# Another order of the constants' allocation in a two-layer encoder trunk

## The chip, the core and the metric

The kernel runs on one core of one Trainium2 chip. The metric is the device time of one execution in microseconds (us); three runs of the kernel before are shown as a median. The profile is of one further execution. TensorE is called PE, VectorE DVE, ScalarE ACT, GpSimd POOL and SyncE SP. PE's loads of the stationary operand have a row of their own, PEld.

## The reference

256 tokens of width 1024 go through two layers. The output is the token matrix, 256 x 1024, float32.

```python
for l in range(DEPTH):                       # DEPTH = 2
    x = x + 0.5 * swiglu(rms_norm(x, ffn1_norm[l]), ffn1_w1[l], ffn1_w3[l], ffn1_w2[l])   # D_FF = 2816
    h = rms_norm(x, mix_norm[l])
    z = h @ w_in[l]                          # 1024 x 6752, split into the inputs of three mixers and 3072 gates
    y_na  = neighborhood_attention(...)      # 8 heads
    y_gla = gla_bidirectional(...)           # 4 heads, gated linear attention in chunks of 64
    y_mla = mla_attention(...)               # 4 heads, low-rank q and kv
    mixed = (gt[:, :, 0] * (y_na @ w_br_na[l]) + gt[:, :, 1] * (y_gla @ w_br_gla[l])
             + gt[:, :, 2] * (y_mla @ w_br_mla[l]))
    x = x + mixed @ w_out[l]
    x = x + 0.5 * swiglu(rms_norm(x, ffn2_norm[l]), ffn2_w1[l], ffn2_w3[l], ffn2_w2[l])
```

## The kernel before

**Split products.** Each float32 operand of a large product is held as two float32r tiles, hi (a rounded copy, made on ACT) and lo (the rest, made on DVE by a subtraction). A product is three matmuls that add up in one bank of PSUM: hi by hi, hi by lo, lo by hi.

**The weight stream.** All weights stand in one list of units of up to 128 x 2048 elements (1 MB) in the order of use. SP loads a unit into one of three buffers `raw`; ACT (L138) and DVE (L144) split it in two halves into one of four buffers `hl`, where `hl[:, 0]` is hi and `hl[:, 1]` is lo. The split runs two units ahead of the matmuls. The order of everything is written out by hand: each function issues its matmuls through the helper `mm` (so they all have line 368) and calls `tick`, which emits a piece of the split and one step of each side task.

**The activations.** `xT` holds the transposed input of the next product: two blocks of 128 tokens (t), hi and lo, eight chunks of 128 features, 16 KB in each partition. It is rewritten after every residual addition (`norm_task`, `mix_task`). Nearly all other intermediate tiles come from a pool `s2` of 31 buffers of 2 KB.

**Which operand stands still.** This differs by stage, and in the rows of the profile `out<-in` the first name behind the arrow is the operand that streams, the second the one that stands still:

- `fform` (the upward half of the feed-forward, 80 calls with 16 pairs of matmuls each): `hl` stands still, 128 columns at a time, and `xT` streams. The first matmul of a pair streams hi and lo of both blocks (512 columns in four runs of 128), the second hi alone (256 columns). In the rows: `acc<-xT,hl`, 128x512 and 128x256.
- `tform` (the first columns of that half, where the norm is not ready yet): `xT` stands still, `hl` streams 256 columns.
- `wide_out` with `uT` (the downward half): `uT`, two buffers of `s2`, stands still, and `hl` streams 512 columns. In the rows: `acc<-hl,s`.
- `dense8` (the input projection of the mixers): `xT` stands still, `hl` streams 512 columns, or 408 in the four groups of gates. In the rows: `acc<-hl,xT`. The small products of the low-rank attention, `up_proj`, stand between them with their operand `cT` in `s2` (`ta<-hl,s`).
- `branch` (the three mixers' outputs): the same helper `burst` as `dense8`, but `yT`, from `s2`, stands still.
- `wide_out` with `X` (the output projection): the same helper as the downward half, but `xT` stands still.

```python
def burst(acc, lh, hl, ks, t, N, start, stop, k0=0):      # dense8: lh = X; branch: lh = yT
    n = len(ks)
    for i, k in enumerate(ks):
        a, b = (i + k0) * N, (i + k0 + 1) * N
        mm(acc, lh(0, k, t), hl[:, 0, a:b], start and i == 0, False)
        mm(acc, lh(0, k, t), hl[:, 1, a:b], False, False)
        mm(acc, lh(1, k, t), hl[:, 0, a:b], False, stop and i == n - 1)
```

**Where the tiles lie.** The pool `cst` hands out addresses in each partition one behind the other, in the order of its allocations, from byte 16512, which is 128 behind a multiple of 512. The pools of `raw`, `hl` and `s2` follow at 65536; all their buffers start on multiples of 512 bytes.

Of the kernel before, what the change touches and what calls it, by code (L numbers as in the profile page):

```python
# [6 lines left out]
F32 = mybir.dt.float32  # L7
F32R = mybir.dt.float32r
BF = mybir.dt.bfloat16
I32 = mybir.dt.int32  # L10
# [35 lines left out]
def body(tc, T):  # L46
# [3 lines left out]
    with ctx:  # L50
        ctx.enter_context(tc.manual_schedule())
        cst = ctx.enter_context(tc.tile_pool(name="cst", bufs=1))
# [17 lines left out]
        tr_t = lambda: bank("ta", 4)  # L70
        at_t = lambda: bank("ta", 4)

# [1 line left out]
        units = []  # L74
        for l in range(DEPTH):
            W = T["layers"][l]
# [91 lines left out]
                if st["hi"] < lim:  # L168
                    emit_hi()

# [1 line left out]
        tasks = []  # L172

        def step(tk):
# [24 lines left out]
            while not tk.done:  # L199
                step(tk)  # L200

# [1 line left out]
        x = cst.tile([128, 2, D], F32, name="x")  # L203
        idt = cst.tile([128, 128], F32, name="idt")
        xT = cst.tile([128, 2, 2, 8, 128], F32R, name="xT")
        gates = cst.tile([128, 2, 2048], F32, name="gates")
        rope = cst.tile([128, 2, 2, 64], F32, name="rope")
        am = cst.tile([128, 64], I32, name="am")
        aT = [cst.tile([128, 2, 2, 128], F32, name=f"aT{t}") for t in range(2)]
        gcol = cst.tile([128, 8], F32, name="gcol")  # L210
        mhalf = cst.tile([128, 16], F32, name="mhalf")
        ones = cst.tile([128, 1], F32, name="ones")
        zT = cst.tile([32, 2, 256], F32R, name="zT")

        def load_consts():
# [171 lines left out]
        def dense8(N, evac, pre=None, between=None):  # L387
            tks = []
            if pre is not None:
                ua, ub = unit(), unit()  # L390
                for t in range(2):
                    for h in range(2):
                        finish(pre[t, h])
                    acc = acc_t()
                    burst(acc[:, :N], X, ua, range(4), t, N, True, False)
                    tick(t == 0)
                    burst(acc[:, :N], X, ub, range(4, 8), t, N, False, True)
                    tks.append(drain(evac, t, acc))
                    tick()
                return tks  # L400
            accs = [acc_t(), acc_t()]
            for kh in range(2):
                u = unit()
                for t in range(2):
                    if kh == 0 and between:
                        between(t)
                    burst(accs[t][:, :N], X, u, range(4 * kh, 4 * kh + 4), t, N, kh == 0, kh == 1)
                    if kh:
                        tks.append(drain(evac, t, accs[t]))
                    tick()  # L410
            return tks
# [32 lines left out]
                for h in range(2):  # L444
                    mm(acc[h], lhs(1, u, kk, t), hl[:, 0, kk * 1024 + h * 512:kk * 1024 + h * 512 + 512], False, e)

# [1 line left out]
        def ffn(norms, after, prefetch, first=None, out=None):  # L448
            uT = {}

# [101 lines left out]

            wide_out(True, lhs, NCH, done)

# [1 line left out]
        def mixer(l, norms, after, prefetch):  # L556
            W = T["layers"][l]
            row, col, gup = params.pop(l)
# [2 lines left out]
            DVE.scalar_tensor_tensor(out=gqk_na, in0=col[:, 0:1], scalar=0.125, in1=col[:, 1:2],  # L561
                                     op0=ALU.mult, op1=ALU.mult)

            # ---- evacuations of the projections
            sg, cn, rl, nqk, nav, gvt, ssr = {}, {}, {}, {}, {}, {}, {}

            def pow_(ss, n):
# [90 lines left out]
                        nc.sync.dma_start(out=nav[j][64 * t + 32 * r:64 * t + 32 * r + 32, :],  # L658
                                            in_=v[64 * r + k0:64 * r + k0 + 32, :])

            # ---- shared by the two softmax attentions
            yT = {}

            def normalise(P, sums):
# [24 lines left out]
                        PE.transpose(ps[:, k, t, :], src[t][:, a:a + 128], idt)  # L689
                return ps.rearrange("p k t n -> p k (t n)")  # L690

            # ---- neighbourhood attention
            naT = {}

            def na_tr(nm, deps):
# [85 lines left out]
                            DVE.tensor_copy(PT, ps)  # L781
                    yield 1

            # ---- latent attention
            mq, mk, mv, mr = {}, {}, {}, {}

            def ev_uq(t, accs):
# [142 lines left out]
                            PTs[h] = p_trans(Ps.pop(h))  # L930
                    yield 1

            # ---- gated linear attention
            gqk = {}
            E, L, Y, dec = {}, {}, {}, {}

# [148 lines left out]
                    ysplit(ps.rearrange("p k n -> p (k n)"), "gla", j)  # L1085
                yield 1

            # ---- projections, with the three mixers running beside them
            m_tk = dense8(512, ev_m, norms)
            c_tk = spawn(c_task(m_tk), 1)  # L1090
            dense8(512, ev_gr)
# [99 lines left out]
                after(t, h)  # L1191
            wide_out(True, lhs, 4, done)

# [1 line left out]
        def spawner(ap, into, params_of=None):  # L1195
            G = []

            def f(t, h):
                into[t, h] = spawn(norm_task(t, h, G[0]), 1)

            def prefetch():
                G.append(load_gain(ap))
                if params_of is not None:
                    load_params(params_of)
            return f, prefetch
# [3 lines left out]
        for l in range(DEPTH):  # L1209
            W = T["layers"][l]  # L1210
            nm, n2 = {}, {}
            ffn(n, *spawner(W["gm"], nm, l), first=first if l == 0 else None)
            mixer(l, nm, *spawner(W["g2"], n2))
            if l + 1 < DEPTH:
                n = {}
                ffn(n2, *spawner(T["layers"][l + 1]["g1"], n))
            else:
                ffn(n2, None, lambda: None, out=T["out"])
# [14 lines left out]


def _rel_index():
    """Row offset, column offset and window test of (block, query, key) in the order of the bands."""
    j, q, p = np.arange(4)[:, None, None], np.arange(64)[:, None], np.arange(128)
    r, c = q % 4, 16 * j + q // 4
    k0 = np.clip(16 * j - 8, 0, 32)
    kr, kc = p // 32, k0 + p % 32  # L1240
    c0 = np.clip(c - 8, 0, 48)
    ok = (kc >= c0) & (kc < c0 + 16)
    dr = np.broadcast_to(kr - r + 7, ok.shape)
    dc = np.clip(kc - c + 15, 0, 30)
    return dr, dc, ok
# [14 lines left out]
def layout(inp):  # L1260
# [6 lines left out]
    j, i = np.arange(128)[:, None], np.arange(128)[None, :]  # L1267
    A["am"] = _tok((j % 64 > i)[:, :64].astype(np.int32))
    dr, dc, ok = _rel_index()
    for l in range(DEPTH):  # L1270
        p = f"l{l}_"
# [68 lines left out]
```

## Time and profile before

| what | value |
|---|---|
| median of 3 runs | 1270.34 us (1270.18 to 1270.63) |
| span of the profiled execution, first to last instruction | 1267.6 us |
| PE busy | 1253.1 us (99%), 7124 matmuls |
| PEld busy | 1074.4 us (85%) |
| DVE busy | 894.0 us (71%) |
| ACT busy | 711.9 us (56%) |
| POOL busy | 221.3 us (17%) |
| DMA | 228.34 MB, mean 180 GB/s |

The profiled execution has its span and no time of its own beside it; the median of the runs is 2.74 us longer than the span, which is the launch and the end around the instructions. Matmuls overlap: one begins while the one before it is still draining, so the duration of one (391 ns) is longer than the step from one start to the next. The step is read from the timeline, where a row that merges n matmuls of one kind gives the time from the first start to the last end: the step is that time less one duration, over n - 1.

### The profile page before, as it was taken

The numbers are of one execution on the slowest core, as the hardware profiler recorded it, in microseconds if no ns is written. First come the engines' busy times: TensorE is split into PE (matmuls) and PEld (weight loads), VectorE is DVE, ScalarE is ACT, GpSimd is POOL, SyncE is SP. The second block draws the span as 40 slices with busy tenths as digits, with TensorE's granted clock in tenths as the row PEclk, the third lists the DMA queues.
The fourth block names the chain that finished last, engine by engine and source line by source line (L and its number), as shares of the span: only waits on it lengthen the run. The fifth ranks groups of instructions, "written<-read, shape, count | busy, mean of one in ns | idle before, by whom it ended". The sixth has DMA issues, their size and how long they took to land.

```text
span 1267.6 us, 18330 instructions
## 1 busy us (share of the span) xinstructions
PE 1253.1 (99%) x7124; PEld 1074.4 (85%) x7124; DVE 894.0 (71%) x1382; ACT 711.9 (56%) x1315; POOL 221.3 (17%) x169
## 2 busy tenths in 40 slices
PE   8999999999999999999999999999999999999998
PEld 7888788889988898888898888888899788988887
DVE  5888736678766878886378886466886567788852
ACT  6555536667665366555365564356686644665541
POOL 0322101132011112220012220021322020122200
PEclk9999999999999999999999999999999999999999
DMA  7655644552543545556355556346526434555561
GB/s 301 222 180 187 241 158 158 203 194 87 196 166 133 200 166 185 185 196 232 133 186 203 195 195 235 113 173 225 167 90 207 163 134 170 196 199 182 186 230 34
DMA packets 37751, 228.34 MB, mean 180 GB/s; under 512 B 5712, under 2 KB 6864, under 8 KB 13088
## 3 DMA queue, kind: packets, MB, share of 16 engines
q1 hardware_dynamic: 37488, 227.09, 50.5%
q8 instruction: 56, 0.92, 0.3%
q14 instruction: 31, 0.25, 0.1%
q0 software_dynamic: 32, 0.07, 0.0%
q10 hardware_dynamic: 144, 0.00, 0.0%
HBM read 224.00 MB, written 1.05 MB: 178 GB/s over the span
## 4 chain that ended last, share of the span: by engine, by line
PE 88%; DVE 7%; ACT 4%; issue 1%; DMA 0%; DVEq 0%; ACTq 0%
PE acc L368 79%; DVE hl L144 6%; PE ta L368 6%; ACT hl L138 2%; ACT s L478 1%; PE ta L689 1%; PE ta L259 1%; DVE s L487 1%; PE ta L776 0%; DVE aT L1017 0%; PE ta L1172 0%; DMA gcol<-in_gcol 0%; PE ta L674 0%; ACT aT L1016 0%; PE ta L608 0%
## 5 line engine op out<-in xcount | busy, mean ns | idle before, releaser
L144 DVE TENSOR_TENSOR hl<-raw,hl 128x1024 fp32r<-128x1024 f32 (+2 forms) x422 | 568.0, 1385 | 101.7 <-ACT hl L138 91.4
L138 ACT ACTIVATE hl<-raw 128x1024 fp32r<-128x1024 f32 (+2 forms) x422 | 417.2, 1041 | 110.2 <-PE acc L368 93.5
L368 PE MATMUL acc<-xT,hl 128*128 128x512 f32 (+1 forms) x2768 | 475.6, 334 | 0.6 <-DVE s L479 0.6
L368 PEld LDWEIGHTS acc<-xT,hl 128*128 128x128 f32 x2768 | 417.8, 188 | 55.7 <-DVE s L479 0.9
L368 PE MATMUL acc<-hl,xT 128*128 128x512 f32 (+2 forms) x1728 | 369.0, 369 | 0.0
L368 PEld LDWEIGHTS acc<-hl,xT 128*128 128x128 f32 x1728 | 299.8, 188 | 45.7 <-issue 2.1
L368 PE MATMUL acc<-hl,s 128*128 128x512 f32 x1344 | 310.9, 391 | 1.5 <-DVE s L479 1.5
L368 PEld LDWEIGHTS acc<-hl,s 128*128 128x128 f32 x1344 | 250.8, 188 | 54.4 <-DVE s L479 1.9
L480 POOL TENSOR_TENSOR s<-s,rsb 128x512 f32<-128x512 f32 x80 | 111.8, 1397 | 355.7 <-DVE s L479 355.7
L489 ACT ACTIVATE s<-s 128x256 fp32r<-128x256 f32 x82 | 34.2, 418 | 172.4 <-DVE s L487 172.4
L479 DVE TENSOR_TENSOR s<-acc,s 128x256 f32<-128x256 f32 x158 | 59.6, 419 | 58.5 <-ACT s L478 58.5
L569 POOL TENSOR_TENSOR sm<-sm,mhalf 128x4 f32<-128x4 f32 (+2 forms) x24 | 36.7, 1531 | 202.7 <-DVE sm L573 196.0
L280 POOL TENSOR_TENSOR sm<-sm,mhalf 128x1 f32<-128x1 f32 x12 | 14.2, 1182 | 298.5 <-DVE sm L279 298.5
L478 ACT ACTIVATE s<-acc 128x256 f32<-128x256 f32 x158 | 50.6, 372 | 0.0
L242 ACT ACTIVATE s<-ta 128x512 fp32r<-128x512 f32 (+1 forms) x46 | 22.9, 531 | 39.9 <-PE ta L689 19.9
L243 DVE TENSOR_TENSOR s<-ta,s 128x512 fp32r<-128x512 f32 (+1 forms) x46 | 26.6, 604 | 24.4 <-ACT s L242 24.1
L368 PE MATMUL ta<-s,s 64*64 64x128 f32 (+3 forms) x720 | 41.0, 265 | 2.1 <-ACT s L1026 2.1
L368 PEld LDWEIGHTS ta<-s,s 64*64 64x64 f32 (+2 forms) x720 | 32.1, 144 | 12.4 <-issue 5.9
L262 ACT ACTIVATE xT<-ta,gain 128x128 fp32r<-128x128 f32 x80 | 22.8, 369 | 35.1 <-PE ta L259 35.1
L485 ACT ACTIVATE s<-s 128x256 f32<-128x256 f32 x82 | 34.2, 418 | 10.9 <-POOL s L480 0.2
L546 DVE SCALAR_TENSOR_TENSOR x<-acc,x 128x512 f32<-128x512 f32 (+1 forms) x20 | 11.3, 579 | 39.7 <-PE acc L368 39.7
L491 DVE TENSOR_TENSOR s<-s,s 128x256 fp32r<-128x256 f32 x82 | 34.0, 415 | 1.9 <-ACT s L489 1.9
(158 smaller groups left out, 652.4 us busy)
## 6 DMA issues: line engine op xcount, KB each, us to landing
raw<-in_l_f_w SPq DMA_DIRECT2D x130, 1024.0 KB, 4.8
raw<-in_l_in_g SPq DMA_DIRECT2D x16, 816.0 KB, 4.4
raw<-in_l_in_late SPq DMA_DIRECT2D x8, 1024.0 KB, 4.8
raw<-in_l_out SPq DMA_DIRECT2D x8, 1024.0 KB, 4.7
raw<-in_l_in_m SPq DMA_DIRECT2D x4, 1024.0 KB, 4.8
raw<-in_l_in_gr SPq DMA_DIRECT2D x4, 1024.0 KB, 4.8
raw<-in_l_in_r SPq DMA_DIRECT2D x4, 1024.0 KB, 4.8
raw<-in_l_in_nv SPq DMA_DIRECT2D x4, 1024.0 KB, 5.0
```

The lines of the kernel that those rows point to most:

```text
L138: ACT.activation(out=hls[j][:, 0, sl], in_=raws[j][:, sl], func=AF.Copy)
L144: DVE.tensor_tensor(out=hl[:, 1, sl], in0=r[:, sl], in1=hl[:, 0, sl].bitcast(F32), op=ALU.subtract)
L242: ACT.activation(out=hi, in_=ps, func=AF.Copy)
L243: DVE.tensor_tensor(out=lo, in0=ps, in1=hi.bitcast(F32), op=ALU.subtract)
L368: PE.matmul(out=out, lhsT=lhsT, rhs=rhs, start=start, stop=stop, skip_group_check=True)
L478: ACT.activation(out=g[:, j, :], in_=a[j][:, 256:], func=AF.Copy)
L479: DVE.tensor_tensor(out=g[:, j, :], in0=a[j][:, :256], in1=g[:, j, :], op=ALU.add)
L480: POOL.tensor_tensor(out=g, in0=g, in1=rb[:, None, :].to_broadcast([128, 2, 256]), op=ALU.mult)
L485: ACT.activation(out=g[:, 0, :], in_=g[:, 0, :], func=AF.Silu)
L489: ACT.activation(out=o[:, 0, :], in_=g[:, 0, :], func=AF.Copy)
L491: DVE.tensor_tensor(out=o[:, 1, :], in0=g[:, 0, :], in1=o[:, 0, :].bitcast(F32), op=ALU.subtract)
L569: POOL.tensor_tensor(out=r[:, :n], in0=ss[:, :n], in1=mhalf[:, :n], op=ALU.pow)
```

## The change

The allocations of the pool `cst` are made in another order: four small tiles first, of 384 bytes together, and the large ones behind them. `ones`, one float wide before, is allocated eight floats wide and used through its first column. Some comments between functions are taken out as well. The core of the diff:

```diff
-        # ---------------- constants ----------------
+        am = cst.tile([128, 64], I32, name="am")
+        mhalf = cst.tile([128, 16], F32, name="mhalf")
+        gcol = cst.tile([128, 8], F32, name="gcol")
+        ones = cst.tile([128, 8], F32, name="ones")[:, :1]
         x = cst.tile([128, 2, D], F32, name="x")
         idt = cst.tile([128, 128], F32, name="idt")
         xT = cst.tile([128, 2, 2, 8, 128], F32R, name="xT")
         gates = cst.tile([128, 2, 2048], F32, name="gates")
         rope = cst.tile([128, 2, 2, 64], F32, name="rope")
-        am = cst.tile([128, 64], I32, name="am")
         aT = [cst.tile([128, 2, 2, 128], F32, name=f"aT{t}") for t in range(2)]
-        gcol = cst.tile([128, 8], F32, name="gcol")
-        mhalf = cst.tile([128, 16], F32, name="mhalf")
-        ones = cst.tile([128, 1], F32, name="ones")
         zT = cst.tile([32, 2, 256], F32R, name="zT")
```

In the two built programs every engine has the same instructions in the same order with the same waits: 10,780 in each, alike but for the step between partitions of `ones` in the few that use it. What differs is the addresses (bytes in each partition):

| tile | bytes | start before | over a multiple of 512 | start after | over a multiple of 512 |
|---|---|---|---|---|---|
| x | 8192 | 16512 | 128 | 16896 | 0 |
| idt | 512 | 24704 | 128 | 25088 | 0 |
| xT | 16384 | 25216 | 128 | 25600 | 0 |
| gates | 16384 | 41600 | 128 | 41984 | 0 |
| rope | 1024 | 57984 | 128 | 58368 | 0 |
| am | 256 | 59008 | 128 | 16512 | 128 |
| aT0, aT1 | 2048 each | 59264 | 384 | 59392 | 0 |
| gcol, mhalf, ones | 32, 64, 4 (32 after) | 63360 | 384 and on | 16768 | 384 and on |
| zT | 2048 | 63488 | 0 | 63488 | 0 |
| raw, hl, s2 | | 65536 and on | 0 | 65536 and on | 0 |

## Rows read from the trace of the kernel before

**Rows 1.** The page: busy time of PE, granted clock by slice, chain by engine.

```profile
PE 1253.1 (99%) x7124; PEld 1074.4 (85%) x7124; DVE 894.0 (71%) x1382; ACT 711.9 (56%) x1315; POOL 221.3 (17%) x169
...
PEclk9999999999999999999999999999999999999999
...
PE 88%; DVE 7%; ACT 4%; issue 1%; DMA 0%; DVEq 0%; ACTq 0%
```

**Rows 2.** Waits of PE, all of them: us in total, times, longest us.

```profile
PE ta L368 <- ACT hl L337: 6.0, 1, 6.0
PE ta L368 <- ACT s L1026: 2.1, 2, 1.1
PE acc L368 <- DVE s L479: 2.1, 2, 1.5
PE ta L1172 <- DVE s L1163: 0.4, 2, 0.2
```

**Rows 3.** Waits of every engine: ACT's split for the matmuls.

```profile
ACT hl L138 <- PE acc L368: 93.5, 29, 3.4
```

**Rows 4.** Matmuls by line and shape: count, then busy us, mean ns of one.

```profile
L368 PE MATMUL acc<-xT,hl 128*128 128x512 f32 x1264 | 444.5, 394 | 0.6 <-DVE s L479 0.6
...
L368 PE MATMUL acc<-hl,s 128*128 128x512 f32 x1344 | 310.9, 391 | 1.5 <-DVE s L479 1.5
L368 PE MATMUL acc<-hl,xT 128*128 128x512 f32 x1056 | 256.9, 398 | 0.0
L368 PE MATMUL acc<-hl,xT 128*128 128x408 f32 x384 | 76.5, 352 | 0.0
L368 PE MATMUL acc<-hl,xT 128*128 128x256 f32 x288 | 35.7, 283 | 0.0
...
L368 PE MATMUL ta<-xT,hl 128*128 128x512 f32 x16 | 5.7, 398 | 0.0
```

**Rows 5.** Timeline of PE, downward half (150 us) and branch (412 us).

```profile
149.82 30.54 PE L368 MATMUL acc<-hl,s 128*128 128x512 f32 x134
...
412.65 8.09 PE L368 MATMUL acc<-hl,s 128*128 128x512 f32 x35
```

**Rows 6.** Timeline of PE, input projection (224 us) and output projection (433 us).

```profile
224.63 7.84 PE L368 MATMUL acc<-hl,xT 128*128 128x512 f32 x33
...
433.61 11.55 PE L368 MATMUL acc<-hl,xT 128*128 128x512 f32 x49
```

**Rows 7.** Timeline of PE, fform (80 us) and tform (455 us).

```profile
79.70 30.59 PE L368 MATMUL acc<-xT,hl 128*128 128x512 f32 x173
...
455.09 8.80 PE L368 MATMUL acc<-hl,xT 128*128 128x256 f32 x72
```

**Rows 8.** Timeline of PE, short runs: up_proj (258 us), gates of 408 columns (348 us).

```profile
258.82 2.94 PE L368 MATMUL ta<-hl,s 128*128 128x512 f32 x12
...
348.17 4.69 PE L368 MATMUL acc<-hl,xT 128*128 128x408 f32 x24
```

**Rows 9.** Loads of the stationary operand, by line.

```profile
L368 PEld LDWEIGHTS acc<-xT,hl 128*128 128x128 f32 x2768 | 417.8, 188 | 55.7 <-DVE s L479 0.9
L368 PEld LDWEIGHTS acc<-hl,xT 128*128 128x128 f32 x1728 | 299.8, 188 | 45.7 <-issue 2.1
L368 PEld LDWEIGHTS acc<-hl,s 128*128 128x128 f32 x1344 | 250.8, 188 | 54.4 <-DVE s L479 1.9 <-issue 0.7
```

**Rows 10.** DVE by line and shape: the same subtraction into s2 and into xT.

```profile
L243 DVE TENSOR_TENSOR s<-ta,s 128x512 fp32r<-128x512 f32 x32 | 20.7, 683 | 11.6 <-ACT s L242 11.6
...
L243 DVE TENSOR_TENSOR xT<-ta,xT 128x512 fp32r<-128x512 f32 x8 | 5.4, 684 | 0.0
```

**Rows 11.** Transposes: PE by line, moving operand idt, stationary x or s2.

```profile
L689 PE MATMUL ta<-idt,s 128*128 128x128 f32 x96 | 13.4, 275 | 0.0
L259 PE MATMUL ta<-idt,x 128*128 128x128 f32 x80 | 12.0, 272 | 0.0
```

**Rows 12.** Busy time by stretch, fform (60 to 110 us): PE, PEld, DVE, ACT, POOL, clock, DMA share.

```profile
60.00:110.00 50.00, 50.00 (x287) 43.83 (x286) 41.92 (x54) 29.54 (x56) 12.66 (x9) 1.00 0.55 190
```

## The prediction

> **What bounds the kernel now.** I read the page first: PE is busy 99% of the span, its clock is granted in full in every slice (the 2.4 GHz level), and the chain that ended last runs through PE for 88% [rows 1]. The waits of PE confirm it: they add up to 10.6 us, of which 6.0 are the first load [rows 2]. ACT's split of the weights, on the other hand, waits 93.5 us for matmuls to free a buffer `hl` [rows 3]: the supply of weights runs ahead and is held back by PE. So the time is the sum of the steps from one matmul to the next, and a change of the step by one nanosecond, over the 4,000 or so matmuls that read `xT` in the large products, is worth 4 us. Nothing else has such leverage, so I read the steps.
>
> A step, from one start to the next, is read from a row of the timeline: (length less one duration) over (count less one). The durations are the means of the shapes.
>
> - Downward half, `uT` in `s2` stands still, `hl` streams 512 columns: (30.54 - 0.391) / 133 = **226.7 ns** [rows 4, 5].
> - Branch, `yT` in `s2` stands still, `hl` streams 512: (8.09 - 0.391) / 34 = **226.4 ns** [rows 4, 5].
> - Input projection, `xT` stands still, `hl` streams 512: (7.84 - 0.398) / 32 = **232.6 ns** [rows 4, 6].
> - Output projection, `xT` stands still, `hl` streams 512: (11.55 - 0.398) / 48 = **232.3 ns** [rows 4, 6].
> - `tform`, `xT` stands still, `hl` streams 256: (8.80 - 0.283) / 71 = **120.0 ns** [rows 4, 7].
> - `fform`: the row begins and ends with the 512-column matmul, so it holds 86 pairs: (30.59 - 0.394) / 86 = **351.1 ns** for 768 columns [rows 4, 7].
>
> The first four are what the reader is to see. Branch and input projection run the same helper, in the same stage, with the same shapes; downward half and output projection share the other helper. The step goes with the tile that stands still, not with the helper or the stage: 226.5 with a tile of `s2`, 232.4 with `xT`. A step of `s2` tiles is also what the columns lead to expect: 226.7 less 120.0 is 106.7 for 256 columns, exactly 2.4 columns per ns. So 512 columns and 256 columns in their undisturbed form make 226.7 + 120.0 = 346.7, and a pair of `fform` is 4.4 ns over that. In `fform` it is `xT` that streams.
>
> **The change part by part.** No instruction is added, removed or moved, no wait is new, and no queue changes; what could change is how long an operand's access takes. `xT` is read in chunks of 128 floats, 512 bytes per partition. Before, every chunk starts 128 bytes over a multiple of 512 and reaches into the next block; after, each lies in one block, as those of `s2` and `hl` always did.
>
> *Input and output projection, 512 columns:* 1056 matmuls [rows 4] at 232.4 against 226.5 is 5.9 ns each, 6.2 us if all of them settle at the step of `s2`. Not all will: after a switch between kinds the steps are longer for a while even with `s2` standing still: `up_proj`, a run of 12, has (2.94 - 0.393) / 11 = 231.5 [rows 8], with the duration of its own form near that of `acc<-hl,s` (391) [rows 4]. Many runs in the projections are that short, because `up_proj` and transposes stand between them. I put half of the matmuls into such runs and give these half of the gain: 4.6 us. Bounds 0 and 6.2.
>
> *Gates, 408 columns:* 384 matmuls [rows 4]. Their step is (4.69 - 0.352) / 23 = 188.6 [rows 8], with one switch in it; by 2.4 columns per ns from 226.7 it would be 183.4. Bounds 0 and 5.2 ns, 0 to 2.0 us; I take 1.0, since the start of the streamed slice, a multiple of 1632 bytes, stays off the blocks either way.
>
> *`fform`:* 1264 and 16 pairs [rows 4] at 4.4 ns is 5.6 us. Bounds 0 and 5.6. Here `xT` is the streamed operand, in four runs of 128 columns, and no row shows such a stream from an aligned tile; I take the upper end, because each run is just one chunk, and the pair then has nothing left that the pair of reference steps has not.
>
> *`tform` and the transposes:* nothing. `tform` takes 120.0 although `xT` stands still in it, so at 256 columns the access is covered. Transposes have durations of 272 and 275 whether `x`, 128 bytes over, or a tile of `s2` stands still [rows 11].
>
> *DVE, ACT, POOL, DMA:* nothing. The same subtraction takes 683 ns into `s2` and 684 into `xT` [rows 10]. `gates`, `rope` and `aT` are read by these engines alone, or by a few dozen matmuls.
>
> Cover: a faster PE must be fed. In `fform` DVE, the busiest feeder, is at 41.92 of 50 us [rows 12]; with PE 1.3% faster it comes to 85%. So nothing late takes the place of the gain.
>
> Sum: 4.6 + 1.0 + 5.6 = 11.2 us off. The span goes from 1267.6 to 1256.4; the median of the runs is 2.74 above the span, which gives **1259.1 us**.
>
> **A rule that speaks against it.** The loads of the stationary operand last 188 ns in all three forms, from `hl`, `s2` and `xT` alike [rows 9]: by themselves they show no cost of the offset. The Trainium skill, page "TensorE: Matmul & The Clock Gate", section "Step-by-step: what each phase is for", says that PE reads its two operands through two independent ports, so that loading the next weights takes nothing from the matmul that runs; and the page "SBUF — State Buffer", section "Door 1: The DMA port swizzle", gives lines of 16 bytes, on which both addresses of `xT` start. By these the sum is nothing and the time stays. The steps of rows 5 and 6 differ all the same by 5.9 ns, so something about `xT` counts; that it is the offset is the likeliest reading, not a shown one.
>
> **The rivals.**
>
> *No effect.* What sets `xT` apart from `s2` may be something else: it lies below 64 KB in the partition, before and after, and its chunks of hi and lo are 4 KB apart. For it: the equal 188 ns, and that `tform` shows no cost. Against it: the operands have the same shape and inner run, and a distance in a partition is a stranger cause than a block that is crossed. Time: 1270.3.
>
> *Only one side gains.* The offset may count for the operand that stands still alone: 4.6 + 1.0 = 5.6, so 1264.7; or for the streamed one alone: 5.6 as well, the same time. For it: `fform`'s excess may come from its four runs or from the change between 512 and 256 columns, neither of which changes.
>
> *Slower.* In `fform` the two operands start 128 bytes apart within a block before and at the same place after. If streams that start alike get in each other's way there, a pair could take the excess that rows 6 show over rows 5 twice, once for each matmul: 11.8 ns over 346.7 is 358.5, 7.4 over now, 9.5 us on 1280 pairs. Less the 5.6 of the other parts that is 1274.2. It decides from the point where a pair grows by 4.4 ns, which eats those 5.6. Against it: in rows 5 both operands start on multiples of 512, and these are the fastest steps.
>
> **How the numbers follow.** Both sides gain: 0.47, between 1255 and 1262. One side: 0.25, around 1264.7. No effect: 0.16, at 1270.3. Slower: 0.12, around 1274. The prediction is that of the likeliest, 1259.1. The range goes from 1255, a little under the sum of all upper bounds (13.8 us, so 1256.5), to 1271, so that the first three cases lie in it; less their tails that is about 0.8. A measurement of this kernel tells about 0.2%, 2.5 us, from no change: faster 0.71, same 0.18, slower 0.11, the last two shared a little between the small and the missing effects.
>
> **What would show it.** The count of instructions and the waits stay. Right: rows like 6 at 226 to 228 per step, a pair of `fform` at 347, `tform` still at 120, rows 5 unmoved. If only rows 6 move, the streamed operand had no part in it; if only `fform` moves, the standing one had none. If rows 6 stay at 232, the offset was not the cause and the prediction is wrong from its first term. If the steps shrink and the span doesn't, some new wait of PE on `hl` must stand in its waits. The prediction would also be wrong if rows 5 grew, whose operands don't move.

## The result, and the profile after

Median of 5 runs 1262.91 us (1262.60 to 1263.80) against 1270.18 us (1268.50 to 1270.63, 5 runs) before: ratio 0.9946, 95% interval 0.9934 to 0.9959. The kernel became 0.54% faster. The span of the profiled execution went from 1267.6 to 1262.0 us.

The two profiled executions are 5.6 us apart, the medians 7.3. In every run that has both, the time is 1.7 to 1.9 us above the span. So the execution profiled before took about 1269.4, less than its median, and the one after, with 1263.80, was the slowest of its five. The stages below account for the 5.6. Of the 2.74 us between median and span before, about 0.9 is this difference and not launch and end; the forecast is the median less 11.2 either way.

The page after, busy time of the engines:

```profile
PE 1246.4 (99%) x7124; PEld 1072.3 (85%) x7124; DVE 894.1 (71%) x1382; ACT 712.6 (56%) x1315; POOL 221.4 (18%) x169
```

PE's busy time fell by 6.7 us at the same 7124 matmuls, while those of DVE, ACT and POOL moved by 0.7 or less [rows 1]. So the steps are next. The timeline of PE after; each row answers to one of rows 5 to 8 (in the order of time: first fform, downward half, input projection, up_proj, gates, branch, output projection, tform, second fform).

```profile
79.82 30.44 PE L369 MATMUL acc<-xT,hl 128*128 128x512 f32 x171
...
149.70 30.54 PE L369 MATMUL acc<-hl,s 128*128 128x512 f32 x134
...
239.37 18.79 PE L369 MATMUL acc<-hl,xT 128*128 128x512 f32 x82
...
258.45 2.88 PE L369 MATMUL ta<-hl,s 128*128 128x512 f32 x12
...
348.09 4.16 PE L369 MATMUL acc<-hl,xT 128*128 128x408 f32 x21
...
410.71 9.46 PE L369 MATMUL acc<-hl,s 128*128 128x512 f32 x41
...
431.82 12.66 PE L369 MATMUL acc<-hl,xT 128*128 128x512 f32 x55
...
454.38 8.40 PE L369 MATMUL acc<-hl,xT 128*128 128x256 f32 x68
...
489.86 20.50 PE L369 MATMUL acc<-xT,hl 128*128 128x512 f32 x117
```

The durations are from the matmuls by line and shape:

```profile
L369 PE MATMUL acc<-xT,hl 128*128 128x512 f32 x1264 | 441.2, 393 | 0.5 <-DVE s L480 0.5
...
L369 PE MATMUL acc<-hl,s 128*128 128x512 f32 x1344 | 310.8, 391 | 1.1 <-DVE s L480 1.1
L369 PE MATMUL acc<-hl,xT 128*128 128x512 f32 x1056 | 252.3, 394 | 0.0
L369 PE MATMUL acc<-hl,xT 128*128 128x408 f32 x384 | 76.8, 353 | 0.0
L369 PE MATMUL acc<-hl,xT 128*128 128x256 f32 x288 | 36.0, 285 | 0.0
```

| product | step before, ns | step after, ns |
|---|---|---|
| downward half | 226.7 | (30.54 - 0.391) / 133 = 226.7 |
| branch | 226.4 | (9.46 - 0.391) / 40 = 226.7 |
| input projection | 232.6 | (18.79 - 0.394) / 81 = 227.1 |
| output projection | 232.3 | (12.66 - 0.394) / 54 = 227.1 |
| up_proj, run of 12 | 231.5 | (2.88 - 0.391) / 11 = 226.3 |
| gates, 408 columns | 188.6 | (4.16 - 0.353) / 20 = 190.4 |
| tform | 120.0 | (8.40 - 0.285) / 67 = 121.1 |
| fform, pair, first feed-forward | 351.1 | (30.44 - 0.393) / 85 = 353.5 |
| fform, pair, second feed-forward | 351.0 | (20.50 - 0.393) / 58 = 346.7 |

(The pair before in the second feed-forward is (20.40 - 0.394) / 57 from the row below.) In their long rows the projections went the whole way. The 512-column matmuls with `xT` standing still lost 256.9 - 252.3 = 4.6 us of busy time. `fform` did so in the second feed-forward, but in the first its pairs grew by 2.4 ns.

Where the time came from is seen by the starts of the stages. Timeline of PE before: first, for the table, the second `fform`; then the long row of the first `fform`, and the starts of the downward halves of the first, second and third feed-forward and of the fourth `fform`:

```profile
490.01 20.40 PE L368 MATMUL acc<-xT,hl 128*128 128x512 f32 x115
...
44.15 90.14 PE L368 MATMUL acc<-xT,hl 128*128 128x512 f32 x512 [0.57 <-DVE s L479]
...
134.12 2.88 PE L368 MATMUL acc<-hl,s 128*128 128x512 f32 x12
138.49 3.79 PE L368 MATMUL acc<-hl,s 128*128 128x512 f32 x15 [1.49 <-DVE s L479]
...
576.73 3.60 PE L368 MATMUL acc<-hl,s 128*128 128x512 f32 x15
...
762.88 7.45 PE L368 MATMUL acc<-hl,s 128*128 128x512 f32 x32
...
1090.70 1.56 PE L368 MATMUL acc<-xT,hl 128*128 128x512 f32 x8
```

The same starts after:

```profile
44.85 90.61 PE L369 MATMUL acc<-xT,hl 128*128 128x512 f32 x512 [0.49 <-DVE s L480]
...
135.30 2.89 PE L369 MATMUL acc<-hl,s 128*128 128x512 f32 x12
139.28 3.10 PE L369 MATMUL acc<-hl,s 128*128 128x512 f32 x12 [1.09 <-DVE s L480]
...
574.80 5.42 PE L369 MATMUL acc<-hl,s 128*128 128x512 f32 x23
...
759.73 6.55 PE L369 MATMUL acc<-hl,s 128*128 128x512 f32 x28
...
1086.38 1.81 PE L369 MATMUL acc<-xT,hl 128*128 128x512 f32 x9
```

The lead over before: 1.18 us behind at the first downward half, 0.79 behind once that half has waited for its last input (a wait of 1.09 instead of 1.49). Of that, 0.70 was there before the long row began (44.85 against 44.15). It doesn't come from the addresses: the last kernel below has those of the changed kernel and begins that row at 44.16. Then 0.71 ahead at `tform` of the second feed-forward (454.38 against 455.09), so the first mixer, with the downward half ahead of it, gave 1.50. Ahead by 1.93 at the second downward half, 3.15 at the third, 4.32 at the fourth `fform`, 5.6 at the end. A settled feed-forward gives some 1.25 us, the second mixer 1.17.

The waits of PE after:

```profile
PE ta L369 <- ACT hl L338: 6.3, 1, 6.3
...
PE acc L369 <- DVE s L480: 1.6, 2, 1.1
PE ta L690 <- DVE s L825: 0.5, 2, 0.2
PE acc L369 <- DVE hl L144: 0.4, 1, 0.4
...
PE ta L777 <- POOL s L771: 0.3, 1, 0.3
```

With the two left out, which are the second and the fourth of [rows 2] and now 2.4 and 0.4 us, they add up to 11.9 us where they were 10.6: three small waits are new. The one on `hl` (0.4) stands at 15.76 us, in the first feed-forward; the other two stand in the mixers and are a part of what these gave back of their 4.6 us.

### The profile page after: what moved, and what is told of

Its sections match the earlier page's. It is cut to its first block, busy times and chain, and to the rows that moved or that the text cites. A ratio compares the mean times of both kernels' runs of the same rounds, so it can differ in the third digit from the quotient of the medians.

```text
span 1262.0 us, 18330 instructions
## 1 busy us (share of the span) xinstructions
PE 1246.4 (99%) x7124; PEld 1072.3 (85%) x7124; DVE 894.1 (71%) x1382; ACT 712.6 (56%) x1315; POOL 221.4 (18%) x169
## 4 chain that ended last, share of the span: by engine, by line
PE 83%; DVE 9%; ACT 4%; DMA 1%; issue 1%; POOL 1%; SPq 0%; DVEq 0%; ACTq 0%; POOLq 0%
PE acc L369 76%; DVE hl L144 7%; PE ta L369 4%; ACT hl L138 2%; DMA raw<-in_l_f_w 1%; ACT s L479 1%; PE ta L690 1%; POOL sm L570 1%; PE ta L260 1%; DVE s L488 1%; DMA s<-in_l_bias 0%; PE ta L777 0%; DVE aT L1018 0%; PE ta L1173 0%; PE ta L675 0%
## 5 line engine op out<-in xcount | busy, mean ns | idle before, releaser
L369 PE MATMUL acc<-hl,xT 128*128 128x512 f32 (+2 forms) x1728 | 365.1, 367 | 0.0
L479 ACT ACTIVATE s<-acc 128x256 f32<-128x256 f32 x158 | 50.7, 372 | 0.0
```

The lines of the kernel that those rows point to most:

```text
L369: PE.matmul(out=out, lhsT=lhsT, rhs=rhs, start=start, stop=stop, skip_group_check=True)
L479: ACT.activation(out=g[:, j, :], in_=a[j][:, 256:], func=AF.Copy)
```

## The experiments

Every edit below moves addresses alone, but the last. The question is what about the address of `xT` counts. **Theory A** is that of the prediction: a chunk of 512 bytes that reaches over a multiple of 512 costs, for each operand by itself. **Theory B**: what counts is the distance between the start of the operand that streams and that of the one that stands still. In the kernel before, the fast rows have a distance of 0 and the slow ones one of 128, so both theories fit it.

The pad of 128 bytes that three of the kernels have is one line ahead of the first `hl`; it moves `hl` and everything behind it, `s2` too, by 128 bytes, and leaves `raw`:

```diff
             st["dma"] = 2
+            wp.tile([128, 32], F32, name="pad")
             hl = hls[0] = wp.tile([128, 2, 2048], F32R, name="hl", tag="hl", bufs=HL_BUFS)
```

**x and idt put back.** The changed kernel with the small tiles between `idt` and `xT`:

```diff
-        am = cst.tile([128, 64], I32, name="am")
-        mhalf = cst.tile([128, 16], F32, name="mhalf")
-        gcol = cst.tile([128, 8], F32, name="gcol")
-        ones = cst.tile([128, 8], F32, name="ones")[:, :1]
         x = cst.tile([128, 2, D], F32, name="x")
         idt = cst.tile([128, 128], F32, name="idt")
+        am = cst.tile([128, 64], I32, name="am")
+        mhalf = cst.tile([128, 16], F32, name="mhalf")
+        gcol = cst.tile([128, 8], F32, name="gcol")
+        ones = cst.tile([128, 8], F32, name="ones")[:, :1]
         xT = cst.tile([128, 2, 2, 8, 128], F32R, name="xT")
```

> The changed kernel with x and idt put back to 128 bytes over a multiple of 512; xT and what lies behind it stays on multiples. If xT alone matters (my theory), the steps are those of the changed kernel: 226.7 ns in the input and output projection, a pair of fform mostly at 347 ns, time 1262 to 1264 us. If x or idt carried a part of the gain, the time goes back towards 1270 and rows of transposes or of x change.

Measured: 1263.70 us, ratio to before 0.9953 (0.9938 to 0.9968). Timeline of PE, input projection and second `fform`:

```profile
239.82 16.51 PE L369 MATMUL acc<-hl,xT 128*128 128x512 f32 x72
...
489.76 20.62 PE L369 MATMUL acc<-xT,hl 128*128 128x256 f32 x118
```

The projection is at (16.51 - 0.394) / 71 = 227.0 ns, and `fform` makes 118 matmuls in 20.62 us, as the changed kernel does in the same stretch (20.61). The gain needs neither `x` nor `idt`; of the tiles that large products read that leaves `xT`.

**Everything 128 bytes over.** The kernel before with the pad: `xT`, `hl` and `s2` all 128 over a multiple of 512.

> The kernel before with 128 bytes put ahead of hl, so that xT, hl and the tiles of s2 all start 128 bytes over a multiple of 512. Theory A, each operand for itself: a chunk that reaches over a multiple of 512 costs whatever the other operand does. Then no product is undisturbed: the downward half and branch (226.7 ns before) go to about 232, which is 1344 x 5.7 = 7.7 us, and with the rest as before the time is about 1278 us. Theory B, the distance between the starts of the two operands within 512 bytes counts: it is 0 everywhere, all steps are those of the changed kernel (226.7 ns, pair 347 ns), time about 1263 us.

Measured: 1263.82 us, ratio 0.9955 (0.9938 to 0.9971). Timeline of PE, downward half, input projection, second `fform`:

```profile
149.77 30.54 PE L369 MATMUL acc<-hl,s 128*128 128x512 f32 x134
...
239.68 16.51 PE L369 MATMUL acc<-hl,xT 128*128 128x512 f32 x72
...
489.84 20.39 PE L369 MATMUL acc<-xT,hl 128*128 128x256 f32 x117
```

Steps: 226.7, (16.51 - 0.394) / 71 = 227.0, pair (20.39 - 0.281) / 58 = 346.7. Every chunk reaches over a multiple of 512 here, `x`, `idt`, `gates` and `rope` lie where they lay before, and the whole gain is there. Theory A falls, and with it the reading of the change as an alignment.

**xT aligned, hl and s2 not.** The changed kernel with the pad.

> The changed kernel with the same 128 bytes ahead of hl: xT on a multiple of 512, hl and s2 128 over one. Theory A: every product has at least one operand that reaches over a multiple: all steps of 512 columns near 232 ns, the downward half too, time 1276 to 1280 us. Theory A for the operand that stands still alone: the projections stay at 226.7 (xT stands still), the downward half and branch go to 232 (s2 stands still), about 1271 us. Theory B: the downward half and branch keep 226.7 (both 128 over), the projections go to 232 and fform back to 351 (128 apart), about 1270 us.

Measured: 1270.26 us, ratio 1.0003 (0.9993 to 1.0012). Timeline of PE, same places:

```profile
149.68 30.54 PE L370 MATMUL acc<-hl,s 128*128 128x512 f32 x134
...
239.84 16.43 PE L370 MATMUL acc<-hl,xT 128*128 128x512 f32 x70
...
489.71 20.53 PE L370 MATMUL acc<-xT,hl 128*128 128x512 f32 x116
```

The downward half, both of whose operands moved, stays at 226.7; the projection is at (16.43 - 0.398) / 69 = 232.3, and `fform` makes 116 matmuls in 20.53 us, exactly the row that the kernel before has in that stretch. `xT` is on a multiple of 512 and nothing is gained. This is theory B in every number.

**A distance of 256.** The changed kernel with `am` behind `aT`, so that `xT` and its neighbours lie 256 bytes over; `hl` and `s2` on multiples.

```diff
-        am = cst.tile([128, 64], I32, name="am")
         mhalf = cst.tile([128, 16], F32, name="mhalf")
...
         aT = [cst.tile([128, 2, 2, 128], F32, name=f"aT{t}") for t in range(2)]
+        am = cst.tile([128, 64], I32, name="am")
```

> The constants in a third order that puts xT (and x, idt, gates, rope, aT) 256 bytes over a multiple of 512; hl and s2 on multiples. If blocks of 512 bytes count (my theory), this is like before: projections near 232 ns, pair of fform near 351, about 1270 us. If multiples of 256 bytes are enough, it is like the changed kernel: 226.7 ns, 347, about 1263 us.

Measured: 1263.07 us, ratio 0.9945 (0.9930 to 0.9960). Timeline of PE, input projection and second `fform`:

```profile
239.73 16.50 PE L369 MATMUL acc<-hl,xT 128*128 128x512 f32 x72
...
489.83 20.39 PE L369 MATMUL acc<-xT,hl 128*128 128x256 f32 x117
```

(16.50 - 0.394) / 71 = 226.8 and a pair of 346.7: a distance of 256 is as good as none.

**The untouched product made slow.** The changed kernel with the pad behind the first `hl` instead, so that `s2` alone is 128 over.

```diff
             hl = hls[0] = wp.tile([128, 2, 2048], F32R, name="hl", tag="hl", bufs=HL_BUFS)
+            wp.tile([128, 32], F32, name="pad")
```

> The changed kernel with 128 bytes put behind hl, so that the tiles of s2 alone are 128 bytes over a multiple of 512; xT and hl are on multiples. Theory B (distance between the two operands): the downward half and branch, whose tiles nobody had touched, now go from 226.7 to about 232.4 ns, while the projections stay at 226.7 and fform at 347. That is 1344 x 5.7 = 7.7 us: about 1270.5 us. Rival: the excess has to do with xT itself (its layout of hi and lo 4 KB apart), not with any pair of operands: the downward half stays at 226.7 and the time at 1263 us.

Measured: 1269.75 us, ratio 0.9998 (0.9989 to 1.0007). Timeline of PE, downward half, input projection, second `fform`:

```profile
149.64 30.61 PE L370 MATMUL acc<-hl,s 128*128 128x512 f32 x131
...
240.26 16.07 PE L370 MATMUL acc<-hl,xT 128*128 128x512 f32 x70
...
489.75 20.61 PE L370 MATMUL acc<-xT,hl 128*128 128x256 f32 x118
```

Now the downward half has (30.61 - 0.396) / 130 = 232.4 ns, while the projection keeps (16.07 - 0.394) / 69 = 227.2 and `fform` the row of the changed kernel. So it is no property of `xT`: `hl` and a tile of `s2` pay the same 5.7 ns in 512 columns when they start 128 bytes apart.

**Distances of 64, either way.** The changed kernel with `mhalf` ahead of `x` and the other small tiles behind `aT` (`xT` 192 over), once with the pad (`hl` and `s2` 128 over, `xT` 64 ahead of them), once without (192 ahead, which is 64 behind within 256).

```diff
-        am = cst.tile([128, 64], I32, name="am")
         mhalf = cst.tile([128, 16], F32, name="mhalf")
-        gcol = cst.tile([128, 8], F32, name="gcol")
-        ones = cst.tile([128, 8], F32, name="ones")[:, :1]
...
         aT = [cst.tile([128, 2, 2, 128], F32, name=f"aT{t}") for t in range(2)]
+        am = cst.tile([128, 64], I32, name="am")
+        gcol = cst.tile([128, 8], F32, name="gcol")
+        ones = cst.tile([128, 8], F32, name="ones")[:, :1]
```

> xT 192 bytes, hl and s2 128 bytes over a multiple of 512: a distance of 64 bytes between xT and hl. 0 and 256 were fast, 128 and 384 slow. If half a step of 256 is the worst case and the cost grows towards it, the projections are between 226.7 and 232.4 ns and the time between 1263 and 1270 us. If any distance off 256 costs the full price, 232 ns and about 1270 us. If only an odd multiple of 128 costs, 226.7 ns and about 1263 us.

> xT 192 bytes over a multiple of 512, hl and s2 on multiples: a distance of 192 bytes, or 64 the other way round within 256. The three cases of the distance of 64 hold here too: between 226.7 and 232.4 ns, or 232 ns and 1270 us, or 226.7 ns and 1263 us. If the order of the two operands matters, this run and that of 64 bytes differ.

Measured: 64 ahead 1271.11 us, ratio 1.0009 (1.0000 to 1.0018); 192 ahead 1269.15 us, ratio 0.9995 (0.9986 to 1.0004). Timeline of PE with 64 ahead, input projection, `tform`, second `fform`:

```profile
239.69 16.49 PE L370 MATMUL acc<-hl,xT 128*128 128x512 f32 x70
...
454.58 8.44 PE L370 MATMUL acc<-hl,xT 128*128 128x256 f32 x72
...
489.63 20.54 PE L370 MATMUL acc<-xT,hl 128*128 128x512 f32 x115
```

And with 192 ahead:

```profile
239.78 16.42 PE L369 MATMUL acc<-hl,xT 128*128 128x512 f32 x71
...
454.09 8.73 PE L369 MATMUL acc<-hl,xT 128*128 128x256 f32 x72
...
489.79 20.54 PE L369 MATMUL acc<-xT,hl 128*128 128x512 f32 x115
```

The projection is at (16.49 - 0.398) / 69 = 233.2 with the tile that stands still 64 ahead, and at (16.42 - 0.395) / 70 = 228.9 with it 64 behind; `fform` is at (20.54 - 0.396) / 57 = 353.4 in the one and at the same in the other. None of the three cases that I had set up holds as it stands: the price is not a slope towards 128, and the sign matters. `tform` at 256 columns goes its own way: (8.44 - 0.278) / 71 = 115.0 and (8.73 - 0.281) / 71 = 119.0, both under the 120.0 of before.

**Four transposes more in the first feed-forward.** To see why `fform` is at 353.5 there and at 346.7 in the second:

```diff
                 fform(i)
+                if first is not None and i == 7:
+                    ps = tr_t()
+                    for k in range(4):
+                        PE.transpose(ps[:, k * 128:k * 128 + 128], idt, idt)
                 if i == 4:
```

> The changed kernel with four transposes of idt more, into a free bank that nobody reads, behind the call of fform for chunk 7 of the first feed-forward; the output is the same. In the changed kernel the pairs of fform run at 347 ns in three of the four feed-forwards, from the four transposes of tform's result on, and at 353 ns in nearly all of the first, which has no such transposes. If an interruption by transposes lets the pairs settle, the pairs behind it, some 220 of 304, go from 353 to 347: 1.4 us off, 0.4 to 0.6 us for the transposes, so 0.8 to 1.0 us below the changed kernel, about 1262 us. If something else in the first feed-forward keeps the pairs at 353 (late weights, loads of constants), the time is 0.5 us above it, about 1263.4 us.

Measured: 1263.78 us (1262.52 to 1265.39), ratio to before 0.9956 (0.9942 to 0.9970); that can't be told from the changed kernel, so the time can't decide between the two cases. Timeline of PE, first `fform` from its start, ahead of the transposes and behind them, and the start of the first downward half:

```profile
44.16 11.38 PE L369 MATMUL acc<-xT,hl 128*128 128x512 f32 x64 [0.48 <-DVE s L480]
...
44.96 10.11 PE L369 MATMUL acc<-xT,hl 128*128 128x512 f32 x57
...
69.68 30.55 PE L369 MATMUL acc<-xT,hl 128*128 128x512 f32 x175
...
133.46 2.91 PE L369 MATMUL acc<-hl,s 128*128 128x512 f32 x12
138.61 3.60 PE L369 MATMUL acc<-hl,s 128*128 128x512 f32 x14 [2.24 <-DVE s L480]
```

Behind the transposes the pairs are at (30.55 - 0.392) / 87 = 346.6 ns. But ahead of them, from the wait at 44 us on, they already are at (10.11 - 0.392) / 28 = 347.1 (the row at 44.96 us, a stretch of the one from 44.16). So this run doesn't show that the transposes moved them. In the kernel with `x` and `idt` put back the pairs change the other way at that wait, from (8.71 - 0.395) / 24 = 346.5 (row at 34.73 us, 49 matmuls) to (11.35 - 0.395) / 31 = 353.4 (row at 45.84 us, 63 matmuls).

What the run does show is where the first feed-forward ends. Its `fform` takes 89.30 us from the start of the long row to that of the downward half (133.46 - 44.16), against 90.45 in the changed kernel (135.30 - 44.85): 1.15 less. The wait for DVE's share of the last chunk (the sum after `fform`, L479 of before) grows from 1.09 to 2.24, by the same 1.15. From the start of the long row to the end of this wait it is 94.34 us before, 94.43 in the changed kernel and 94.45 here, with pairs at 351, 353.5 and 347. So the first feed-forward ends by its DVE work, not by PE, and the step of its pairs is worth nothing there.

## Why the prediction was right, and where not

The time, 1262.9, lies in the range and on the forecast side, 3.8 us above the 1259.1 of the likeliest case. Of the 11.2 us, 7.3 came. That is nearer to the 1264.7 of the rival in which only one side gains; the rows decide against this rival, since the projections and the second `fform` both moved. The first reading stands but for the first feed-forward: the kernel is the sum of PE's steps, and the step depends on where two tiles lie.

**The mechanism was not the one predicted.** The prediction took the multiple of 512, and the block that a chunk reaches over, for the cause. The cause is the distance of the two operands, 0 or 256 against 128: shown by the kernel with all three 128 over (gain without alignment), by the one with `xT` alone aligned (alignment without gain), and by the one that makes the downward half slow. For this change both readings give the same steps, because `hl` lay on multiples. That is luck: with `hl` and `s2` 128 over, the same place of `xT` gave 1270.26, no gain. The pair of 346.7 was luck in part too: its 120.0 came from a product whose operands lie 128 apart, and that one takes 121.1 at distance 0. The argument against the rival of streams that get in each other's way when they start alike, that rows 5 start alike and are the fastest, was sound, and that rival is out: starting alike is what is fast (the pairs of the first `fform` did grow, but by 2.4 ns, and at no cost in time). The rival without effect is out too, with its grounds of an address below 64 KB and of hi and lo 4 KB apart, which are the same before and after.

**Projections, 4.6 us: right in size of the steps.** Busy time fell by 4.6, and summed over the trace from one start to the next, within runs of one kind, the gain is 4.36. Short runs behind transposes keep about half of the excess, as supposed. The same 12 matmuls behind four transposes in the timeline of PE before, and then after:

```profile
214.81 3.04 PE L368 MATMUL acc<-hl,xT 128*128 128x512 f32 x12
```

```profile
215.24 3.00 PE L369 MATMUL acc<-hl,xT 128*128 128x512 f32 x12
```

That is (3.04 - 0.398) / 11 = 240.2 and (3.00 - 0.394) / 11 = 236.9 ns, a gain of 3.3 of 5.9. `up_proj` between projections, on the other hand, gained 5.2 ns, although neither of its operands moved; that fits a step which it inherited from its neighbours before, and not the cost of a switch that the prediction read in its 231.5. What failed is the way from the steps to the end: the two mixers, the first with the downward half ahead of it, brought the start of the next stage forward by 1.50 and 1.17 us, 2.7 of the 4.6. The same sums say where the rest went: 0.33 lost in the gates, 0.24 in the products of 256 columns, which became about 1 ns slower per step, and 1.28 in the last steps of the runs of 512 and 408 columns, which hold the new small waits; `up_proj` added 0.18.

**Gates, 1.0 us: a small loss.** The busy time of the 408-column matmuls went from 76.5 to 76.8 us, and the step in the table grew from 188.6 to 190.4. Summed as above, they lost 0.33 us within their runs. Their slices of `hl` start 1632 bytes apart, so their distance to `xT` changes with every chunk, before and after.

**`fform`, 5.6 us: mis-sized, the largest miss.** It gave about 1.25 us in each of three feed-forwards, 3.7 in all, where 960 pairs at 4.4 ns are 4.2. The 304 pairs of the first, 1.3 us in the prediction, gave nothing: the 0.79 that it lost are the 0.70 of its late start and 0.09 behind it. I had taken the upper end because nothing would be left that the reference steps have not. What was left is a second stable step, 353 ns, in which the pairs can stay at a distance of 0. What decides which of the two they fall into was not found.

**Cover.** That DVE at 85% hides nothing was wrong for one place, the end of the first feed-forward. There DVE's work for the last chunk ends last, before and after: PE goes on 94.3 to 94.5 us after the long row began, whether its pairs take 347, 351 or 353.5 ns. That is why the first quarter of `fform` is missing.

**The rule that spoke against it.** The Trainium skill, page "TensorE: Matmul & The Clock Gate", section "Step-by-step: what each phase is for", has the two operands read through independent ports. By it, moving one operand by 128 bytes should change nothing, and the loads do last the same after, as [rows 9] had them. Loads of the stationary operand by line, after:

```profile
L369 PEld LDWEIGHTS acc<-hl,xT 128*128 128x128 f32 x1728 | 299.8, 189 | 42.4 <-issue 2.1
```

But the steps don't agree: in the downward half, 226.7 and 232.4 ns with nothing changed but 128 bytes of distance.

## What to carry to other kernels

When PE is busy all the time, read its step from long rows of the timeline and compare products of the same shape: two that differ by 2% with the same helper differ by their operands. Look at the addresses of both operands, not at one: here a distance of 0 or 256 bytes between the starts, in place of 128, was worth 5.7 ns in each 512-column matmul, and moving either tile restored or removed it. A gain of PE arrives only where PE ends the stage last; in the first feed-forward a faster step became a longer wait for DVE.

## What the runs showed of the hardware that was not expected

With float32r operands and 512 streamed columns at the full clock (mean granted 0.999 to 1.0 in each profile), the step in long rows was 226.4 to 227.2 ns when the stationary operand and the streamed one start 0 or 256 bytes apart, 232.3 to 232.6 at 128 either way, 233.2 with the stationary one 64 ahead and 228.9 with it 64 behind (within 256). With 256 columns the order is another: `tform` takes 121.1 at distance 0 (the changed kernel), 120.0 at 128, 119.0 and 115.0 at 64 behind and ahead. So no one distance is best for both widths.

What in the array or its reads makes these steps is not settled by these runs.
